# First norm and projections: modulation weights loaded by pairs of features with 1 KB rows, both token halves accumulated in six banks, values computed behind all features

## The chip, the cores and the metric

The kernel runs on one NeuronCore of a Trainium2 chip. The metric is the device time of one execution in microseconds (us). The core has five engines, each with an instruction stream of its own: TensorE (PE, matmuls, with its weight loads shown as PEld), VectorE (DVE), ScalarE (ACT), GpSimd (POOL) and SyncE (SP, which issues nearly all transfers). Tiles live in the on-chip memory with 128 partitions; matmuls write to eight banks of accumulators, each 128 partitions by 512 float32 elements.

## The reference

A trunk of two layers over 1024 tokens with 1024 channels, in float32. Each layer norms its input, modulates it, mixes tokens (layer 0: attention with a forget gate; layer 1: gated linear attention), and then runs a norm, a modulation and a gated feed-forward part. The change lies in the first norm, the first modulation and the first projections of layer 0:

```python
def rms_norm(x, g):
    y = xf * lax.rsqrt(jnp.mean(xf * xf, axis=-1, keepdims=True) + EPS)
    return (y * g).astype(x.dtype)

def modulate(h, shift, scale):
    return h * (1.0 + scale[:, None, :]) + shift[:, None, :]
...
...
def forgetting_attention(h, w_in, b_f, w_out):
    proj = h @ w_in
    q, k, v, f_logit = jnp.split(proj, [D_MODEL, 2 * D_MODEL, 3 * D_MODEL], axis=-1)
    ...
    log_f = jax.nn.log_sigmoid(f_logit.astype(jnp.float32) + b_f.astype(jnp.float32))
    cum = jnp.cumsum(log_f, axis=1).transpose(0, 2, 1)
    ...
        logits = logits + cum[:, :, qs:qe, None] - cum[:, :, None, :qe]
```

The modulation of a layer comes from `mod = c_act @ ada_w[i] + ada_b[i]`: six vectors of 1024, shift, scale and gate for the mixer and the same three for the feed-forward part. There are 16 heads of 64 channels, so a pair of heads is 128 channels.

## The kernel before, in words

**Numbers.** Every float32 matrix is held as a pair: a high part in the reduced format that TensorE takes, and a low part, the difference. A product is three matmuls, high by high, high by low and low by high (`mm3`, lines 241 to 243). A weight is loaded (`load_w`, L198), cast to its high part in two pieces on ACT (L206), and its low part is made in four pieces, three on POOL and one on DVE (L209).

**Features and tokens.** "Feature" d is a block of 128 of the 1024 channels, 0 to 7. Tokens come in two halves of 512. `xt[0]` to `xt[7]` hold x, 128 tokens each. `h` is held transposed: `hT[d]` has feature d on the partitions and tokens along the row.

**The first stage** does this:

- `load_x` fetches x, `load_ada0(d)` the first two modulation vectors' weights of feature d: two tiles, each with two transfers of 256 KB whose rows are 128 floats, 512 bytes (L288). There are 32 such transfers.
- `ss_half(hf)` norms one half of the tokens: squares with row sums on ACT (L456), the mean on DVE (L458), the power -1/2 on POOL (L459), and the scaling of each `xt` on DVE, ACT or POOL (L463, L465, L467). All four scalings of the second half are on POOL.
- `ada0_mod(d)` makes shift and scale of feature d: for features 0 to 2 half of the sum over the 1024 inputs goes on TensorE as products with `cact` (L479), the rest, and all of it for features 3 to 7, is accumulated on DVE over tiles of 256 columns (L485, L487), and its partitions are summed by a product with `ones` (L489). Then `modc` (L490) and `amul` (`make_a`, L351).
- `h_block(d, hf)` transposes x of that feature on TensorE (L496), applies scale and shift on ACT (`y_s`, L498), casts to the high part on ACT (L500), and makes the low part on DVE for even d, on POOL for odd (L501).
- `first_k(d, hf, acc)` adds feature d to three accumulators, each in a bank of its own: the forget gate `fs_b` (L508, L509), and the first query and key pair `qs_b`, `ks_b`.
- `first_v(d)` adds feature d to the values of the first token half, in two more banks, one feature behind `first_k` (`VLAG = 1`).
- `first_evac` takes the accumulators out: the gate through a sum of the gate's parts, an absolute value, an exponential and, after the second half, a logarithm, the scan over tokens (L803) and a round trip to memory from which `load_cum` (L821) brings the sums back for each head; then the query and key copies.
- `v_split` copies values out of their bank as a pair: cast on ACT (L163), difference on DVE (L164).

The first half of the tokens runs through all eight features first (the loop `for d in range(8)` with `pre(d + 1)`), with x of the second half loaded and normed at d = 4; then the second half runs through all eight. The banks of the first stage are divided by `ps_rings(5, 2, 1)`: five for accumulators (`par`), two for transposes, one for modulation products. Afterwards the banks are divided anew: two (`pj`) for projections, the others for scores, transposes and outputs of attention.

**Behind the first stage.** `run(v_half(0, 1))` computes the values of the second token half in the two `pj` banks (`vps_b`, lines 241 to 243). Then seven rounds follow: round p runs attention of head pair p (scores `s_b`, transposes, outputs `o_b`) woven with the query and key projections of pair p + 1 (`qk_b`, `qk_proj`), and in rounds 0 to 5 with half of the values of a later group. At the end of each `qk_proj` the call `ada0(3.0)` issues so much of the rest of layer 0's modulation (`ada_steps`: loads L369, accumulation on DVE in `acc_s`, L386 and L388, in steps of one unit): the other four of the six vectors, which are needed after attention.

**What sets the order.** The code is written as a sequence; a scheduler then lays the instructions out for each engine by dependences and its own estimate of when each could start, so an instruction that is written later can stand earlier on its engine. `tc.issue_after(ins)` keeps the instructions written under it behind `ins`. Rings (`Ring`, `take`) hand out slots of memory in turn: the next tile of a ring waits for the last reader of the tile that had its slot. SP issues transfers in its own order, and a transfer that waits for a slot holds up those behind it.

## Time and profile before

| | |
|---|---|
| median of 3 runs | 2428.96 us (2426.21 to 2429.33) |
| the profiled execution | 2424.66 us, of which the profile's span is 2422.8 us |
| granted TensorE clock, mean | 0.994 |
| TensorE busy | 2369.6 us (98%), 12344 matmuls |
| DVE busy | 1772.8 us (73%) |
| ACT busy | 1130.3 us (47%) |
| POOL busy | 1025.2 us (42%) |
| moved by DMA | 359.24 MB, mean 148 GB/s |

How to read the rows that follow: times are in us from the span's start. A line such as `58.93 1.33 DVE L487 ... x1` in the timeline is an instruction (or several alike, xN) with its start, its duration, engine, line of the code, operation, output tile, inputs and shape; brackets at its end give the idle time of the engine before it and what ended that wait. In rows of groups the two numbers behind the bar are the busy time in us and the mean duration of one in ns; behind the next bar stands the idle time of the engine just before them. "busy" for TensorE includes times at which it runs at a lower granted clock. The TensorE clock that is granted stands as a share of full speed.

### The profile page before, as it was taken

To read this page: it belongs to the slowest core of one execution; us is meant where nothing else is said; L and a number is where in the kernel's file an instruction comes from. 1 tells how busy PE (TensorE), PEld (TensorE's weight loads), DVE (VectorE), ACT (ScalarE), POOL (GpSimd) and SP (SyncE) were. 2 spreads that over 40 slices of the span, in tenths; PEclk is the share of its full clock that TensorE was granted. 3 is DMA by queue.
4 is the path that set the end of the run, shared out by engine and by line. 5 is a ranking of instruction groups with operands and counts; after the bars stand their busy time and mean duration, and the time that the engine had idled before them with its cause. 6 is when DMAs were issued, how large, how long until landed. Compare 5 with 4: busy or idle time off the path is not lost.

```text
span 2422.8 us, 35876 instructions
## 1 busy us (share of the span) xinstructions
PE 2369.6 (98%) x12344; PEld 2015.4 (83%) x12344; DVE 1772.8 (73%) x3044; ACT 1130.3 (47%) x2186; POOL 1025.2 (42%) x922
## 2 busy tenths in 40 slices
...
GB/s 272 80 88 107 93 115 103 91 88 105 126 96 200 169 166 174 153 181 259 228 213 176 61 126 97 114 116 168 109 92 178 157 133 154 133 169 262 226 205 148
DMA packets 348959, 359.24 MB, mean 148 GB/s; under 512 B 24221, under 2 KB 293689, under 8 KB 348777
## 3 DMA queue, kind: packets, MB, share of 16 engines
...
q14 instruction: 86, 0.70, 0.1%
...
## 4 chain that ended last, share of the span: by engine, by line
PE 81%; DVE 7%; DMA 4%; SPq 2%; ACT 2%; issue 2%; POOL 1%; DVEq 0%; POOLq 0%; ACTq 0%
PE p_b L243 16%; PE p_b L242 16%; PE p_b L241 16%; PE o_b L964 2%; PE t_b L950 2%; PE qk_b L241 2%; PE qk_b L242 2%; PE qk_b L243 2%; SPq L369 1%; DMA ad_s<-in_ada_w_dram 1%; PE s_b L919 1%; PE s_b L920 1%; PE vps_b L241 1%; PE vps_b L243 1%; PE vps_b L242 1%
## 5 line engine op out<-in xcount | busy, mean ns | idle before, releaser
L164 DVE TENSOR_TENSOR o_s<-xv_s,o_s 128x512 fp32r<-128x512 f32 (+1 forms) x376 | 321.8, 859 | 59.0 <-ACT o_s L163 58.3
L163 ACT CAST o_s<-xv_s 128x512 fp32r<-128x512 f32 (+1 forms) x376 | 217.1, 587 | 311.6 <-PE p_b L243 256.4
L242 PE MATMUL p_b<-B,o_s 128*128 128x512 f32 x608 | 236.9, 390 | 0.0
L243 PE MATMUL p_b<-B,o_s 128*128 128x512 f32 x608 | 236.5, 389 | 0.0
L241 PE MATMUL p_b<-B,o_s 128*128 128x512 f32 x608 | 235.5, 390 | 0.0
L930 POOL TENSOR_SCALAR lp_s<-lp_s,st 128x128 f32<-128x128 f32 (+7 forms) x128 | 97.5, 766 | 301.8 <-DVE st L929 260.3
L700 POOL TENSOR_TENSOR ex_s<-xv_s,xv_s 128x512 f32<-128x512 f32 (+1 forms) x64 | 86.3, 1349 | 274.8 <-DMA xv_s<-in_ffn_w_in_dram 104.0
L242 PE MATMUL p_b<-T,o_s 128*128 128x512 f32 x480 | 186.9, 389 | 0.0
L241 PE MATMUL p_b<-T,o_s 128*128 128x512 f32 x480 | 186.9, 389 | 0.0
L243 PE MATMUL p_b<-T,o_s 128*128 128x512 f32 x480 | 181.2, 390 | 0.0
L243 PEld LDWEIGHTS p_b<-B,o_s 128*128 128x128 f32 x608 | 114.1, 188 | 23.7
L242 PEld LDWEIGHTS p_b<-B,o_s 128*128 128x128 f32 x608 | 114.2, 188 | 23.6
L241 PEld LDWEIGHTS p_b<-B,o_s 128*128 128x128 f32 x608 | 114.2, 188 | 23.5
L928 ACT ACTIVATE lp_s<-lp_s,st 128x128 f32<-128x128 f32 (+7 forms) x128 | 99.3, 776 | 69.2 <-DVE st L924 66.7
L702 POOL TENSOR_TENSOR xv_s<-ex_s,xv_s 128x512 f32<-128x512 f32 (+1 forms) x64 | 84.4, 1319 | 67.2 <-DVE o_s L164 65.0
L163 ACT CAST pt_s<-t_b 128x512 fp32r<-128x512 f32 (+1 forms) x160 | 79.5, 547 | 70.4 <-PE t_b L950 69.6
L1303 DVE TENSOR_TENSOR ex_s<-ex_s,p_b 128x512 f32<-128x512 f32 x140 | 93.6, 680 | 24.2 <-PE p_b L243 24.1
L242 PEld LDWEIGHTS p_b<-T,o_s 128*128 128x128 f32 x480 | 90.1, 188 | 18.7
L241 PEld LDWEIGHTS p_b<-T,o_s 128*128 128x128 f32 x480 | 90.1, 188 | 18.7
L243 PEld LDWEIGHTS p_b<-T,o_s 128*128 128x128 f32 x480 | 90.1, 188 | 18.6
L164 DVE TENSOR_TENSOR pt_s<-t_b,pt_s 128x512 fp32r<-128x512 f32 (+1 forms) x160 | 96.3, 631 | 11.1 <-ACT pt_s L163 10.9
L924 DVE CUSTOM_DVE_ANT_0 lp_s<-s_b,cum_s 128x512 f32<-128x512 f32 (+3 forms) x128 | 72.2, 569 | 41.3 <-PE t_b L950 23.7
...
## 6 DMA issues: line engine op xcount, KB each, us to landing
...
ada_s<-in_ada_w_dram SPq DMA_DIRECT2D x128, 128.0 KB, 2.8
...
```

Of the source, the lines that this page charges most:

```text
L163: nc.scalar.copy(hi, src)
L164: nc.vector.tensor_sub(lo, src, hi.bitcast(F32))
L241: nc.tensor.matmul(ps, ah, bh, start=start, stop=False)
L242: nc.tensor.matmul(ps, ah, bl, start=False, stop=False)
L243: nc.tensor.matmul(ps, al, bh, start=False, stop=stop)
L700: nc.gpsimd.tensor_add(s1, a21, a22)
L702: nc.gpsimd.tensor_sub(a11, s1, a11)
L924: nc.vector.tensor_tensor_reduce(lp[:, k0:k1], ps, cm[:, k0:k1], 1.0, mcur, ALU.add, ALU.min, mnew)
L928: nc.scalar.activation(lp, lp, AF.Exp, bias=mcur, scale=-1.0, accum_out=st[:, qi, 2:3])
L930: nc.gpsimd.tensor_scalar(lp, lp, st[:, qi, 3:4], 1.0, op0=ALU.mult, op1=ALU.mult)
L950: nc.tensor.transpose(tp[:, i, :], lps[qi][:, psl(2 * b + jj)], ident)
L1303: nc.vector.tensor_add(d, d if src is None else dest(G, src), ps)
```

## The change

- The weights of the first modulation are loaded by pairs of features (`d2`, 0 to 3): a tile has two of the eight input blocks, and its rows are 256 floats, 1 KB. The pieces are 256 KB as before, and there are 32 as before. Their order on SP's queue changes: x of the second half comes behind pair 1, ahead of pairs 2 and 3; both value weights come behind pair 3.
- Shift and scale are made for a pair at a time. Only pair 0 has a part on TensorE (two of eight input blocks); the rest is accumulated on DVE, in tiles of 512 columns, into two `acc2` views that take one slot from the `wst` ring.
- The first accumulation of a pair is kept behind the last low part of an even feature that was written before it (`lo_ins`), the first product of pairs 1 to 3 behind the last TensorE instruction written before it, the squares of the second half behind ACT's last instruction, and the splits of the value weights behind the last instruction of each engine at that point (`split_after`).
- The banks are divided 6, 1, 1. Both token halves have their three accumulators at once, and the loop runs over pairs: pair d2 of the first half, then pair d2 - 1 of the second half. The last pair of the second half comes at the end.
- `first_v` is gone: the values of both halves are computed by `v_half(0, 0)` and `v_half(0, 1)` in the two `pj` banks, behind all features.
- The scalings of the second half are spread as those of the first: two on DVE, one on ACT, one on POOL.
- The rest of layer 0's modulation is left out of round 0 and issued at 3.5 instead of 3.0 for each call from round 1 on.

```diff
@@ -201,13 +201,21 @@
         flat = lambda t: t.rearrange("p k m -> p (k m)")
         hi, lo, rw = flat(w.hi), flat(w.lo), flat(raw)
         n = kk * m
+        def behind(e):
+            return tc.issue_after(split_after[e]) if split_after else ExitStack()
         for i in range(2):
             cs = slice(i * n // 2, (i + 1) * n // 2)
-            nc.scalar.copy(hi[:, cs], rw[:, cs])
+            with behind("A"):
+                nc.scalar.copy(hi[:, cs], rw[:, cs])
         for i in range(4):
             cs = slice(i * n // 4, (i + 1) * n // 4)
-            (nc.gpsimd if i < 3 else nc.vector).tensor_sub(lo[:, cs], rw[:, cs], hi[:, cs].bitcast(F32))
+            with behind("G" if i < 3 else "D"):
+                (nc.gpsimd if i < 3 else nc.vector).tensor_sub(lo[:, cs], rw[:, cs], hi[:, cs].bitcast(F32))
         return w
+    split_after = {}
 
     def load_w16(src, name, ws=ws):
 
@@ -270,23 +278,25 @@
     mrows = take(4)
     adr = Ring(big, adr_sl + mrows[1:] + acc_sl + s1_sl)
     mrows = Views(mrows[:1], 8, [P], "mrows").v
-    wst = Ring(big, take(6))
-    par, tp0, mp0 = ps_rings(5, 2, 1)
+    wst = Ring(big, take(5))
+    acc2 = Views(take(1), 2, [2, 256], "acc2")
+    par, tp0, mp0 = ps_rings(6, 1, 1)
 
     xt = [xr([P, D], F32, f"xt{t}") for t in range(8)]
 
     def load_x(t):
         nc.sync.dma_start(xt[t], x[0, psl(t), :])
 
-    adaw = ada_w.rearrange("l (k p) (j d m) -> l p k j d m", p=P, j=6, m=P)
+    adaw = ada_w.rearrange("l (k p) (j d m) -> l p k j d m", p=P, j=6, m=256)
     araw = {}
 
-    def load_ada0(d):
-        for kh in range(2):
-            t = adr([P, 4, 2, P], F32, f"adas{d}{kh}")
+    def load_ada0(d2):
+        for kq in range(4):
+            t = adr([P, 2, 2, 256], F32, f"adas{d2}{kq}")
             for j in range(2):
-                nc.sync.dma_start(t[:, :, j, :], adaw[0, :, 4 * kh:4 * kh + 4, j, d, :])
-            araw[(d, kh)] = t
+                nc.sync.dma_start(t[:, :, j, :], adaw[0, :, 2 * kq:2 * kq + 2, j, d2, :])
+            araw[(d2, kq)] = t
 
     load_x(0)
     rows2 = mrows[1][0:32]
@@ -312,7 +322,8 @@
     wq0 = load_w(W[:, 0:P], "wq0", wst)
     wk0 = load_w(W[:, D:D + P], "wk0", wst)
     load_ada0(1)
-    load_ada0(2)
+    for t in range(4, 8):
+        load_x(t)
 
 
     crep = [yv.v[3][0:8, psl(t)] for t in range(4)] + [mrows[4][0:16, :], mrows[5][0:16, :]]
@@ -450,45 +461,50 @@
 
     hT = new_h("h0")
 
-    def ss_half(hf):
+    def ss_half(hf, after=None):
         for t in range(4 * hf, 4 * hf + 4):
             sq = sqr([P, D], BF16, f"sq{t}")
-            nc.scalar.activation(sq, xt[t], AF.Square, accum_out=ssx[:, t:t + 1])
+            with tc.issue_after(after) if after else ExitStack():
+                nc.scalar.activation(sq, xt[t], AF.Square, accum_out=ssx[:, t:t + 1])
         cs = slice(4 * hf, 4 * hf + 4)
         nc.vector.tensor_scalar(rstd[:, cs], ssx[:, cs], 1.0 / D, EPS, op0=ALU.mult, op1=ALU.add)
         nc.gpsimd.tensor_tensor(rstd[:, cs], rstd[:, cs], mhalf[:, 0:4], op=ALU.pow)
         for t in range(4 * hf, 4 * hf + 4):
             r = rstd[:, t:t + 1]
-            if hf == 0 and t % 2 == 0:
+            if t % 2 == 0:
                 nc.vector.tensor_scalar(xt[t], xt[t], r, None, op0=ALU.mult)
-            elif hf == 0 and t == 1:
+            elif t % 4 == 1:
                 nc.scalar.activation(xt[t], xt[t], AF.Copy, scale=r)
             else:
                 nc.gpsimd.tensor_scalar(xt[t], xt[t], r, 1.0, op0=ALU.mult, op1=ALU.mult)
 
-    VLAG, XD = 1, 4
-    NPE = (4, 4, 4, 0, 0, 0, 0, 0)
-    def ada0_mod(d):
-        npe = NPE[d]
-        mp = mp0([P, 2], F32, f"mp{d}")
-        part = lambda k: araw[(d, k // 4)][:, k % 4]
-        for j in range(2):
-            for k in range(npe):
-                nc.tensor.matmul(mp[:, j:j + 1], part(k)[:, j, :], cact[:, k:k + 1], start=k == 0 and j == 0,
-                                 stop=k == 7 and j == 1)
-        if npe < 8:
-            acc = sm.tile([P, 2, P], F32, tag="t1k", name=f"acc0{d}")
+    NPE = (2, 0, 0, 0)
+    def ada0_mod(d2, after_d, after_p):
+        npe = NPE[d2]
+        mp = mp0([P, 2, 2], F32, f"mp{d2}")
+        part = lambda k: araw[(d2, k // 2)][:, k % 2]
+        acc = acc2()
         for k in range(npe, 8):
             if k == npe:
-                nc.vector.tensor_scalar(acc, part(k), cact[:, k:k + 1], None, op0=ALU.mult)
+                with ExitStack() as es:
+                    if after_d:
+                        es.enter_context(tc.issue_after(after_d))
+                    nc.vector.tensor_scalar(acc, part(k), cact[:, k:k + 1], None, op0=ALU.mult)
             else:
                 nc.vector.scalar_tensor_tensor(acc, part(k), cact[:, k:k + 1], acc, op0=ALU.mult, op1=ALU.add)
-        for j in range(2 if npe < 8 else 0):
-            nc.tensor.matmul(mp[:, j:j + 1], acc[:, j, :], ones, start=npe == 0, stop=npe == 0 or j == 1)
-        nc.vector.tensor_add(modc[:, 0, 0:2, d], mp, vec[:, d:d + 16:8])
-        make_a(0, 0, slice(d, d + 1))
+        prods = [(j, i, part(k)[:, j, psl(i)], cact[:, k:k + 1]) for j in range(2) for i in range(2) for k in range(npe)]
+        prods += [(j, i, acc[:, j, psl(i)], ones) for j in range(2) for i in range(2)]
+        for n, (j, i, w, v) in enumerate(prods):
+            with ExitStack() as es:
+                if after_p and n == 0:
+                    es.enter_context(tc.issue_after(after_p))
+                nc.tensor.matmul(mp[:, j, i:i + 1], w, v, start=n == 0, stop=n == len(prods) - 1)
+        ds_ = slice(2 * d2, 2 * d2 + 2)
+        nc.vector.tensor_add(modc[:, 0, 0:2, ds_], mp,
+                             vec[:, 0:16].rearrange("p (j d) -> p j d", j=2)[:, :, ds_])
+        make_a(0, 0, ds_)
 
     def h_block(d, hf):
         tp = tp0([P, HALF], F32, f"xp{d}{hf}")
@@ -499,6 +515,13 @@
         hi, lo = hT[d].hi[:, hsl(hf)], hT[d].lo[:, hsl(hf)]
         nc.scalar.copy(hi, y)
         (nc.gpsimd if d % 2 == 1 else nc.vector).tensor_sub(lo, y, hi.bitcast(F32))
+        if d % 2 == 0:
+            lo_ins.append(last_ins())
+    lo_ins = []
+    def last_ins():
+        return nc.cur_bb.bb.instructions[-1]
 
     def first_acc(hf):
         return [(w, par([P, HALF], F32, f"{nm}s{hf}")) for nm, w in (("f", wf), ("q", wq0), ("k", wk0))]
@@ -510,9 +533,6 @@
         for w, ps in acc[1:]:
             mm3(ps, w.hi[:, d, :], w.lo[:, d, :], hT[d].hi[:, hsl(hf)], hT[d].lo[:, hsl(hf)], d == 0, d == 7)
 
-    def last_ins():
-        return nc.cur_bb.bb.instructions[-1]
 
     sp_ins, rb_ins = [], []
     LATE1 = 7
@@ -820,55 +840,44 @@
         cums[h] = cumr([P, S], F32, f"cum{h}")
         nc.sync.dma_start(cums[h], cum_d[h].partition_broadcast(P))
 
-    vts[0] = []
     ss_half(0)
-    acc = first_acc(0)
-    vacc = [par([P, 2, 256], F32, f"vps0{tp}") for tp in range(2)]
-    def first_v(d):
-        wv = wvs[0][d // 4]
-        for tp in range(2):
-            for i in range(2):
-                ts_ = psl(2 * tp + i)
-                p_, a_ = vacc[tp][:, i, :], (hT[d].hi[:, ts_], hT[d].lo[:, ts_])
-                nc.tensor.matmul(p_, a_[0], wv.hi[:, d % 4, :], start=d == 0 and i == 0, stop=False)
-                nc.tensor.matmul(p_, a_[0], wv.lo[:, d % 4, :], start=False, stop=False)
-                nc.tensor.matmul(p_, a_[1], wv.hi[:, d % 4, :], start=False, stop=d == 7 and i == 1)
-    def pre(d):
-        ada0_mod(d)
-        if d + 3 < 8:
-            load_ada0(d + 3)
-        h_block(d, 0)
-    pre(0)
-    for d in range(8):
-        if d == 0:
-            feed.depth = 1
-            wvs[0] = [feed.next()]
-        if d == 2:
-            wvs[0].append(feed.next())
-        if d < 7:
-            pre(d + 1)
-        first_k(d, 0, acc)
-        if d >= VLAG:
-            first_v(d - VLAG)
-        if d == XD:
-            for t in range(4, 8):
-                load_x(t)
-            ss_half(1)
-    for d in range(8 - VLAG, 8):
-        first_v(d)
-    first_evac(0, acc)
-    acc = first_acc(1)
-    for tp in range(2):
-        v_split(0, tp, vacc[tp])
-    h_block(0, 1)
-    for d in range(8):
-        if d < 7:
-            h_block(d + 1, 1)
-        first_k(d, 1, acc)
-    first_evac(1, acc)
+    accs = [first_acc(hf) for hf in range(2)]
+    def last_of(e):
+        return next(i for i in reversed(nc.cur_bb.bb.instructions) if i.engine == ENG[e])
+    def blocks(d2, hf):
+        for d in (2 * d2, 2 * d2 + 1):
+            h_block(d, hf)
+    def firsts(d2, hf):
+        for d in (2 * d2, 2 * d2 + 1):
+            first_k(d, hf, accs[hf])
+    feed.depth = 1
+    for d2 in range(4):
+        ada0_mod(d2, lo_ins and lo_ins[-1], d2 and last_of("P"))
+        if d2 < 2:
+            load_ada0(d2 + 2)
+        blocks(d2, 0)
+        if d2 == 1:
+            ss_half(1, last_of("A"))
+        if d2 == 3:
+            split_after.update((e, last_of(e)) for e in "ADG")
+            wvs[0] = [feed.next(), feed.next()]
+        firsts(d2, 0)
+        if d2 == 0:
+            continue
+        if d2 == 3:
+            first_evac(0, accs[0])
+        blocks(d2 - 1, 1)
+        firsts(d2 - 1, 1)
+    blocks(3, 1)
+    firsts(3, 1)
+    split_after.update((e, last_of(e)) for e in "ADG")
+    first_evac(1, accs[1])
     def v_half(g, half):
 
         if g not in vts:
@@ -893,7 +902,8 @@
             ps = pj([P, HALF], F32, f"qk{i}{p}{hf}")
             yield from proj(ps, wt, hT, hf)
             (k_evac if i else q_evac)(ps, qkt[p], hf)
-        ada0(3.0)
+        if p > 1:
+            ada0(3.5)
 
     oTs = {}
 
@@ -1008,6 +1018,7 @@
     acc0 = acc_r([P, 2, HALF], F32, "acc0")[:, 0, 0:256]
     for j in (2, 3, 4, 5):
         ada0.q.append(ada_steps(0, j, acc0, wr, 4, 0))
+    run(v_half(0, 0))
     run(v_half(0, 1))
     for p in range(7):
         parts = [qk_proj(p + 1, 0), qk_proj(p + 1, 1)]
```

## The prediction

> **What bounds the kernel now.** I read the page first, then the busy time by stretch over the start of the kernel, then the timeline there. The page gives the profiled execution's span and shows TensorE as the chain that ends last.
>
> ```profile
> span 2422.8 us, 35876 instructions
> PE 81%; DVE 7%; DMA 4%; SPq 2%; ACT 2%; issue 2%; POOL 1%; DVEq 0%; POOLq 0%; ACTq 0%
> ```
>
> The change lies in the first norm and the projections behind it, so what matters is how much of that stage is not TensorE work. The table by stretch (busy us of PE, PEld, DVE, ACT, POOL with their counts, then granted clock, DMA share, GB/s):
>
> ```profile
> 22.00:38.00 16.00, 15.34 (x70) 13.67 (x71) 11.81 (x27) 3.83 (x6) 5.36 (x7) 0.79 1.16 299
> 38.00:56.80 18.80, 17.28 (x108) 14.73 (x107) 15.67 (x39) 10.85 (x19) 7.00 (x8) 1.00 1.12 304
> 56.80:66.90 10.10, 2.57 (x11) 1.51 (x9) 9.44 (x13) 1.78 (x4) 7.95 (x8) 0.59 0.16 40
> 66.90:78.90 12.00, 11.98 (x61) 10.65 (x61) 8.04 (x15) 7.42 (x13) 2.56 (x2) 0.78 0.56 166
> 78.90:108.20 29.30, 29.28 (x189) 26.21 (x187) 11.51 (x19) 20.37 (x35) 5.04 (x5) 1.00 0.07 19
> 108.20:110.80 2.60, 0.00 (x0) 0.00 (x0) 2.60 (x4) 1.26 (x3) 2.60 (x1) 1.00 0.01 3
> 130.00:140.00 10.00, 7.78 (x65) 7.45 (x64) 6.44 (x17) 4.72 (x12) 1.79 (x3) 1.00 0.22 68
> 165.00:465.00 300.00, 295.70 (x1966) 261.78 (x1965) 237.34 (x621) 183.52 (x404) 111.06 (x154) 1.00 0.34 104
> ```
>
> Up to 56.8 us the DMA engines are full (share 1.12 to 1.16). Then comes a hole: 2.57 us of TensorE work in 10.1. From 66.9 to 108.2 TensorE is full, and from 165 it is full again (295.7 of 300). What can be won is therefore the hole, the pause at 108.2 and the 2.2 us missing at 130 to 140. The timeline says who makes them:
>
> ```profile
> 56.25 4.99 POOL L467 TENSOR_SCALAR xt_s<-xt_s,rstd 128x1024 f32<-128x1024 f32 x4
> 58.17 0.84 DVE L386 TENSOR_SCALAR acc_s<-ada_s,c 128x256 f32<-128x256 f32 x1 [0.29 <-DMA ada_s<-in_ada_w_dram]
> 58.93 1.33 DVE L487 SCALAR_TENSOR_TENSOR acc<-adas_s,cact,acc 128x256 f32<-128x256 f32 x1
> 64.19 0.99 PE L489 MATMUL mp_b<-ones,acc 128*128 128x1 f32 x4 [4.80 <-DVE acc L487]
> 110.83 0.47 PE L241 MATMUL qk_b<-h0h,w_h_s 128*128 128x512 f32 x1 [2.65 <-DVE v_s L164]
> 132.82 0.48 DVE L388 SCALAR_TENSOR_TENSOR acc_s<-ada_s,c,acc_s 128x256 f32<-128x256 f32 x1 [3.41 <-DMA ada_s<-in_ada_w_dram]
> 134.48 0.62 PE L964 MATMUL o_b<-pt_s,v_s 128*128 128x256 f32 x3 [2.22 <-DVE pt_s L164]
> ```
>
> The modulation of feature 7 is late on DVE, because the layer's other modulation (L386, L388) has slipped between its steps and the four scalings on POOL slow DVE (1.33 us for an operation that takes 0.48 alone). At 132.8 DVE stands 3.41 us for a load of that same other modulation, and TensorE with it. The pause before 110.83 is the copying of values out of the two `pj` banks.
>
> **The change part by part.** I place the changed kernel on the same clock and ask when `qk_b` starts (110.83 now), with everything ahead of it done in both. A granted clock of 1.00 stands in the rows below unless I say otherwise.
>
> *Loads.* The queue is the same up to x3, which lands at 10.74. The 32 pieces of 256 KB stay 32 pieces, with half the rows.
>
> ```profile
> 10.74 1.06 ACT L456 ACTIVATE sq_s<-xt_s 128x1024 bf16<-128x1024 f32 x1 [0.16 <-DMA xt_s<-in_x_dram]
> 18.61 1.14 ACT L206 CAST wk0h_s<-wk_s 128x512 fp32r<-128x512 f32 x2 [0.67 <-DMA wk_s<-in_fox_w_in_dram]
> 25.92 0.35 DVE L485 TENSOR_SCALAR acc<-adas_s,cact 128x256 f32<-128x256 f32 x1 [1.71 <-DMA adas_s<-in_ada_w_dram]
> 30.95 1.14 ACT L206 CAST wv_0h_s<-wv_s 128x512 fp32r<-128x512 f32 x2 [1.44 <-DMA wv_s<-in_fox_w_in_dram]
> GB/s 0 199 198 344 180 360 361 308 244 227 281 300 291 291 290 291 291 290 293 336 300 294 294 291 300 333 297 289 292 358 405 412 378 305 291 203 181 203 149 17
> ```
>
> From wk (18.61) to the end of feature 2's weights (25.92) eight pieces with 512 B rows land: 0.91 us each. Then four more such (3.65 us) and the 512 KB of `wv`, whose rows are 1 KB, end at 30.95: 1.4 us, 0.70 us per 256 KB. The x rows (4 KB) run at about 405 GB/s, 1.3 us each (the last line, in slices of 1.5 us). So 0.75 us a piece, between 0.70 and 0.91: pair 0 is in at 16.7, the forget, query and key weights at 21, pair 1 at 27, x4 to x7 at 32, pair 2 at 38, pair 3 at 44, the value weights at 47. SP now passes x4 to x7 ahead of pairs 2 and 3, and both value loads behind everything; they were in the middle. The Trainium skill (DMA: Bandwidth & Descriptors, Specifications) gives 512 B as the least transfer for line rate, by which the wider rows bring nothing; the rows here show 0.91 against 0.70, and by its rule pair 0 would be in 1.3 us later.
>
> *DVE work for the modulation.* 8 + 44 operations on 256 columns become 4 + 26 on 512, and TensorE's products with `cact` go from 24 to 8.
>
> ```profile
> L487 DVE SCALAR_TENSOR_TENSOR acc<-adas_s,cact,acc 128x256 f32<-128x256 f32 x44 | 24.6, 569 | 0.9
> L485 DVE TENSOR_SCALAR acc<-adas_s,cact 128x256 f32<-128x256 f32 x8 | 3.5, 434 | 2.2 <-DMA adas_s<-in_ada_w_dram 2.1
> L1167 DVE SCALAR_TENSOR_TENSOR B<-ya_s,modc,B 128x512 fp32r<-128x512 f32 x16 | 11.2, 744 | 0.0
> 43.13 0.50 PE L489 MATMUL mp_b<-ones,acc 128*128 128x1 f32 x4
> L498 ACT ACTIVATE y_s<-xp_b,modc,amul 128x512 f32<-128x512 f32 x16 | 12.2, 774 | 27.8 <-DVE amul L351 24.5 <-PE xp_b L496 3.4
> L500 ACT CAST h0h<-y_s 128x512 fp32r<-128x512 f32 x16 | 9.7, 617 | 0.2
> L456 ACT ACTIVATE sq_s<-xt_s 128x1024 bf16<-128x1024 f32 x8 | 8.4, 1056 | 3.7 <-DMA xt_s<-in_x_dram 3.5
> L463 DVE TENSOR_SCALAR xt_s<-xt_s,rstd 128x1024 f32<-128x1024 f32 x2 | 2.3, 1186 | 1.1 <-POOL rstd L459 1.1
> L459 POOL TENSOR_TENSOR rstd<-rstd,mhalf 128x4 f32<-128x4 f32 x2 | 2.0, 1025 | 16.7 <-DVE rstd L458 16.7
> ```
>
> A 512-column step takes 0.75 us undisturbed, a first one I put at 0.55 (between 0.43 and 0.74). In sum 28.1 us become 26 x 0.75 + 4 x 0.55 = 21.7 us, a gain on an engine that is not the bound. What counts is where they stand. In the order of the built program pair p's sum starts only behind the low part of the last even feature, and its `ones` products stand in TensorE's queue behind the projections before it. So a pair costs in series: sum 0.55 + 7 x 0.75 = 5.8, products 0.95 (four, two of which take 0.50), `modc` and `amul` 0.35, `y` 0.78, `h` 0.62, handovers 0.3: 8.8 us from the release of the sum to the first projection.
>
> *The chain up to the last pair.* Pair 0: scaling of x ends 15.5 as now, sum of six steps and a small split 4.6, products at half clock 1.8, a weight split and the small operations 1.0: `y` at 23, low part at 24.7. Pair 1's sum 24.7 to 30.5 (its last piece landed at 27); with products and the rest `h` of feature 2 is there at 34.2, of 3 at 35.7. The squares of x4 to x7 are ordered behind that cast on ACT: 4 x 1.18 = 4.7, `rstd` 0.2, power 1.03, two scalings on DVE 2.3: x4 to x7 are ready at 44, though they landed at 32. Behind TensorE's transposes of them stands everything else, so it pauses from 38.3 to 44.1. The low part of feature 0 of the second half is done at 46.9, and only then pair 2's sum (its weights wait since 38): 52.7. `h` of 4 at 55.5; 5, then 2 of the second half, low part at 60.2. Pair 3's sum: 66.0; `h` of feature 6, and with it the last projections, at 69.
>
> *From there to `qk_b`.*
>
> ```profile
> 93.79 0.40 PE L508 MATMUL fs_b<-h0h,fw_s 128*128 128x512 f32 x1
> 95.62 0.28 PE L242 MATMUL vps_b<-wv_4l_s,h0h 128*128 128x256 f32 x1
> 101.05 0.28 PE L241 MATMUL vps_b<-wv_0h_s,h0h 128*128 128x256 f32 x1
> 107.29 0.28 PE L243 MATMUL vps_b<-wv_4h_s,h0l 128*128 128x256 f32 x1
> 31.65 2.34 POOL L209 TENSOR_TENSOR wv_0l_s<-wv_s,wv_0h_s 128x256 fp32r<-128x256 f32 x3 [2.62 <-ACT wv_0h_s L206]
> 98.19 0.58 ACT L223 COPY ze_s<-fs_b 16x512 f32<-16x512 f32 x1 [4.91 <-PE fs_b L509]
> 107.32 0.42 DVE L164 TENSOR_TENSOR v_s<-vps_b,v_s 128x256 fp32r<-128x256 f32 x1
> ```
>
> A feature's projections take 1.83 us (eight matmuls, 93.79 to 95.62), a value product 0.12 us (52 of them, 101.05 to 107.29). At 69 there remain 6 features (11.0), 5 sets of transposes (2.3), all 192 value products (23.0) and the first scores (0.65): 36.9 us. Three stalls come on top. The value weights are split behind the last casts of the first half, on ACT and then POOL (2.34 us for three quarters): 1.4 us before the cover of other products is there. The third value product needs the bank whose copying out stands on DVE behind the forget gate's chain: 98.19 to 107.74 now, 9.6 us and one more cast of 0.37, against 69 products (8.3 us) that cover it: 1.7 us. Sum: 69 + 36.9 + 3.1 = 109.0 us, 1.8 us ahead of 110.83. That last stall replaces the 2.65 us of now, since `qk_b` finds its bank free.
>
> What the sum leaves out: POOL slows DVE where both run (0.569 on average against 0.48 undisturbed for the same step above). A low part or a weight split on POOL of about 1.35 us falls on each of pairs 1 to 3; at 1.75 times the duration that is 0.6 to 1.0 us per pair, 2.2 us. And the clock: from 69.12 to 72.10 below seven matmuls take 0.43 us each instead of 0.23, after the hole.
>
> ```profile
> 69.12 0.63 PE L242 MATMUL qs_b<-h0l,wq0h_s 128*128 128x512 f32 x1
> 72.10 0.47 PE L242 MATMUL qs_b<-h0l,wq0h_s 128*128 128x512 f32 x1
> ```
>
> After the pause of 5.8 us I expect the same once, 1.7 us, of which pair 2's sum hides most (TensorE waits 2.35 us for it); I take 0.5. So `qk_b` at 111.7, 0.9 us later than now. Bounds: 0.70 and 0.68 for the DVE step and no disturbance give 107.5, everything disturbed and half clock after each pause 118.
>
> *The other modulation.* Its steps leave the first stage and the first of the seven attention rounds, and go at 3.5 instead of 3.0 a call into the other six. The 2.2 us at 134.48 vanish; what returns is a sixth more of it in rounds in which TensorE is busy 98.6% and DVE 79%: bounds 0 and 2 us, taken 0.5, nearest to the 4.3 us that all causes cost TensorE in those 300 us.
>
> *At no cost.* Six banks for `par` and one each for transposes and modulation: the transposes of the next feature wait for ACT's `y`, which the projections of the one before cover (1.83 against 0.78 + 0.62). `wst` loses a slot to `acc2`; its value halves go to slots of their own as before.
>
> Sum: +0.9 - 2.2 + 0.5 = -0.8 us. The profiled execution took 2424.66 us (2422.8 and 1.9 around it), 4.3 below the median of the runs, 2428.96. So 2423.9 in a profile like that, **2428 us** in the median: no change that can be measured (0.2%, 4.9 us, is about what a measurement of this kernel can tell).
>
> **The rivals.**
>
> *Faster, about 2421 us.* The pauses are shorter than I make them: steps undisturbed (-2.2), the clock never drops (-0.5), the value weights are split in time (-1.4), and without the other modulation the first rounds run freer than the 2.2 us (another 2 us). Sum -6.9, some 2422, or 2421 with 0.68 us a step. For it: DVE has 6.4 us less to do, the gate chain ends 5 us earlier against the scores. Against it: the pauses at pairs 1 to 3 are in the order, not in the load.
>
> *Slower, about 2435 us: the half clock.* After each pause TensorE runs about 3.6 us at half clock, 1.7 us lost. Places: from the start up to 38 (0.79 granted in 22 to 38 now, in spite of 15.34 us of work in 16), after 38.3 to 44.1, before pair 2 and before pair 3: four times 1.7, 6.8 us, of which nothing is hidden if DVE is disturbed as well. Then `qk_b` starts at 111.2 + 6.8 = 118, sum +7.2 - 2.2 + 0.5 = +5.5 to +7 us. It decides from the point where the pauses at pairs 2 and 3 (3.6 us each with the products in them) count as idle. The Trainium skill (TensorE: Matmul & The Clock Gate, Part 1: The HAM clock gate) says that an idle window of about 3.4 us brings the half clock and a busy one takes it away; the hole and the 3.6 us after it agree. By that rule the pause of 5.8 us drops the clock for certain and those of pairs 2 and 3 may.
>
> *The change does not do what it says:* the rows of 1 KB bring nothing, 0.91 us a piece. Then pair 0 is 1.3 us later, pair 1's sum only 0.5, since it waits for DVE by then: +1 us, 2429, inside the forecast.
>
> **How the numbers follow.** The forecast (with the last rival) 0.37, faster 0.33, slower 0.30. The forecast's own range is 2424 to 2433; the cases on both sides hold most of the chance, so the range reaches past both by what the six later rounds may add, a microsecond each, since another order of the start shifts what collides in them: 2421 - 6 = 2415 to 2435 + 6 = 2441.
>
> **What would show it.** TensorE idle some 6 us around 38 to 44 behind POOL or DVE `xt`, and 2 us in front of the `ones` products of pairs 2 and 3; no L388 step before 165; `qk_b` between 109 and 114; no gap of 2 us near 134. It is wrong if pair 2's sum is not behind the second half's scaling, if half-clock rows stand after 55, or if the rounds from 165 on differ by more than 2 us.

## The result

| | before | changed |
|---|---|---|
| median | 2429.47 us (2426.21 to 2430.78, 6 runs) | 2439.23 us (2435.11 to 2441.93, 6 runs) |
| profiled execution | 2424.66 us, span 2422.8 us | 2439.18 us, span 2437.2 us |
| granted clock, mean | 0.994 | 0.991 |

The ratio is 1.0039, with a 95% interval of 1.0026 to 1.0052: the change costs 9.8 us, where 2428 us and no measurable change had been forecast. The page of the changed kernel, its span and its chain of waits by engine:

```profile
span 2437.2 us, 35771 instructions
...
PE 78%; DVE 9%; DMA 5%; ACT 3%; issue 2%; SPq 2%; POOL 1%; DVEq 0%; POOLq 0%; ACTq 0%
```

TensorE still ends last, with more of the chain on DVE, ACT and DMA. The stretches that the prediction showed of before, now of the changed kernel (busy us of PE, PEld, DVE, ACT, POOL with counts, granted clock, DMA share, GB/s):

```profile
22.00:38.00 16.00, 12.06 (x47) 9.21 (x47) 9.29 (x14) 6.91 (x11) 6.41 (x8) 1.00 1.07 368
38.00:56.80 18.80, 10.53 (x42) 7.59 (x41) 10.03 (x14) 7.70 (x12) 4.50 (x4) 0.82 0.57 174
56.80:66.90 10.10, 9.81 (x43) 7.82 (x43) 4.40 (x6) 5.02 (x8) 2.69 (x2) 0.83 0.00 0
66.90:78.90 12.00, 8.35 (x32) 6.83 (x33) 5.34 (x10) 5.03 (x9) 3.08 (x5) 0.72 0.00 1
78.90:108.20 29.30, 28.48 (x205) 26.55 (x204) 13.77 (x22) 22.20 (x36) 9.03 (x11) 1.00 0.19 55
...
130.00:165.00 35.00, 34.15 (x248) 31.34 (x247) 23.48 (x66) 20.29 (x47) 15.79 (x23) 1.00 0.24 73
165.00:465.00 300.00, 293.80 (x1944) 260.52 (x1943) 241.99 (x624) 178.61 (x393) 107.51 (x148) 0.99 0.35 108
```

The hole at 57 to 67 us is filled, but 8.3 us are missing at 38 to 56.8 and 3.7 at 67 to 79, both with a clock below 1. From 130 to 165 TensorE is fuller than before (34.15 against 32.78 us), from 165 to 465 emptier (293.80 against 295.70). TensorE's timeline names the waits:

```profile
43.50 0.78 PE L512 MATMUL xp_b<-ident,xt_s 128*128 128x128 f32 x2 [3.98 <-DVE xt_s L475]
...
54.68 1.05 PE L503 MATMUL mp_b<-ones,acc_s 128*128 128x1 f32 x8 [1.60 <-DVE acc_s L496]
...
70.66 1.73 PE L503 MATMUL mp_b<-ones,acc_s 128*128 128x1 f32 x8 [2.28 <-DVE acc_s L496]
...
113.58 0.40 PE L249 MATMUL qk_b<-h0h,w_h_s 128*128 128x512 f32 x1
```

`qk_b` starts at 113.58 instead of 110.83, only 2.75 us later. So most of the 14.5 us between the two profiled executions arises behind the stage that was changed. To see where, I took the starts of the same matmuls in both traces and the median of their differences in stretches of 20 us, on the clock of the kernel before (us later than in the first profile of before; minus is earlier; the rows below the first are the experiments' profiles):

| kernel | 200 | 300 | 400 | 480 | 560 | 600 | 660 | 1000 | 1600 | 2000 | 2400 |
|---|---|---|---|---|---|---|---|---|---|---|---|
| changed | 0.4 | 1.0 | 1.2 | 5.3 | 5.7 | 10.2 | 10.2 | 11.8 | 11.9 | 15.1 | 14.4 |
| before_again | 0.1 | -0.1 | -0.1 | -0.1 | 0.2 | 0.3 | 0.3 | 2.0 | 1.9 | 4.2 | 3.8 |
| after_again | 3.2 | 3.7 | 3.8 | 7.7 | 7.7 | 11.5 | 11.5 | 13.2 | 14.2 | 15.9 | 15.3 |
| after_pace3 | 4.9 | 4.8 | 4.7 | 4.8 | 6.1 | 7.3 | 7.3 | 10.7 | 10.7 | 10.9 | 10.2 |
| before_pace35 | -4.7 | -4.2 | -3.9 | -0.2 | 0.0 | 0.2 | 0.2 | 0.2 | 1.1 | 2.7 | 2.8 |
| before_skip0 | -5.1 | -5.1 | -6.5 | -4.6 | -2.5 | -2.0 | -1.6 | 0.0 | 0.5 | 1.9 | 2.1 |
| after_pad | 2.7 | 3.2 | 3.2 | 6.9 | 6.6 | 6.8 | 6.8 | 6.8 | 5.8 | 7.3 | 7.6 |
| after_warm | 2.5 | 3.0 | 2.8 | 6.3 | 6.1 | 6.0 | 6.0 | 9.2 | 8.8 | 9.5 | 9.2 |
| after_sq | -5.6 | -5.1 | -4.7 | -0.2 | -0.2 | 4.2 | 4.2 | 5.8 | 8.6 | 6.5 | 5.3 |
| after_sq_acc | -6.2 | -5.7 | -5.3 | -1.3 | -1.5 | 2.8 | 2.8 | 4.4 | 4.9 | 4.3 | 3.4 |
| mix35 | -6.8 | -4.0 | -3.4 | -0.7 | -1.2 | -1.1 | -1.1 | -1.1 | 1.2 | 2.5 | 2.1 |
| mix_skip30 | -7.4 | -7.4 | -8.8 | -6.6 | -3.8 | -3.3 | -3.0 | -2.9 | -4.3 | -2.9 | -3.5 |
| mix30 | -7.1 | -7.3 | -7.3 | -7.4 | -7.6 | -7.6 | -7.6 | -4.3 | -4.0 | -1.0 | -1.1 |

The changed kernel's lag has three steps: 4 us between 400 and 480, 4.5 between 560 and 600, and some 4 behind 660. Each is taken up below. (A value stands for the 20 us from the time at the head of its column.)

**The step at 430.** The timeline of the changed kernel, rows of SP, DVE and TensorE:

```profile
420.56 10.61 SPq L380 DMA_DIRECT2D ada_s<-in_ada_w_dram  x12
...
426.51 3.60 DVE L399 SCALAR_TENSOR_TENSOR acc_s<-ada_s,c,acc_s 128x256 f32<-128x256 f32 x7
...
433.43 0.48 DVE L399 SCALAR_TENSOR_TENSOR acc_s<-ada_s,c,acc_s 128x256 f32<-128x256 f32 x1 [1.98 <-DMA ada_s<-in_ada_w_dram]
...
436.15 0.90 PE L960 MATMUL t_b<-ident,lp_s 128*128 128x128 f32 x3 [2.26 <-POOL lp_s L940]
```

Three loads of the other modulation, twelve pieces, stand in a row on SP; DVE works through seven steps, then stands 1.98 us for a load, the reciprocals for POOL's `lp_s` stand behind that, and TensorE waits 2.26 us. In the kernel before the same transposes follow without a wait:

```profile
431.98 0.52 PE L950 MATMUL t_b<-ident,lp_s 128*128 128x128 f32 x3
```

**The step at 586.** Attention's output of a group is written to memory (`oT_d`) and read back (`or_s`) for the output projection. The timeline (rows of SP, ACT and TensorE), and below it the DMA view of 574.4 to 581.5 us (queue; then issues with KB and us to landing), all of the changed kernel:

```profile
574.45 0.48 SPq L1001 DMA_DIRECT2D oT_d<-oT_s  x1
...
581.49 0.34 SPq L1047 DMA_DIRECT2D or_s<-oT_d  x1
...
585.06 1.04 ACT L163 CAST ohh<-or_s 128x1024 fp32r<-128x1024 f32 x1 [3.68 <-DMA or_s<-oT_d]
...
586.64 0.58 PE L974 MATMUL o_b<-pt_s,v_s 128*128 128x256 f32 x1 [2.40 <-ACT pt_s L163]
```

```profile
q1 hardware_dynamic: 672, 1.05, 43.5%
q8 instruction: 1, 0.02, 0.8%
...
oT_d<-oT_s SPq DMA_DIRECT2D x1, 512.0 KB, 7.0
```

The same view of before, from the write's issue to that of the reading back (568.71 to 573.75):

```profile
q1 hardware_dynamic: 672, 1.05, 65.9%
...
oT_d<-oT_s SPq DMA_DIRECT2D x1, 512.0 KB, 5.0
```

The write landed 7.0 us after its issue; in before it was 5.0. One packet lies in it that before does not have there: 16 KB of instructions on queue 8, from 578.39 to 579.33 us in the trace. ACT's cast of `or_s`, which has to come first, is late, `pt_s` behind it too, and TensorE waits 2.40 us.

**The steps behind 660** have no wait. These are the stretches at half clock of the changed kernel, and below them the window of 3.41 us ahead of four of them:

```profile
43.53:50.35 6.82, 5.29 (x15) 3.80 (x16) 4.47 (x6) 3.01 (x5) 1.99 (x2) 0.50 0.69 198
57.18:60.59 3.41, 3.41 (x11) 2.82 (x12) 0.69 (x1) 1.87 (x3) 0.95 (x1) 0.50 0.00 0
70.83:77.66 6.83, 5.51 (x20) 4.74 (x21) 1.01 (x3) 3.79 (x7) 1.72 (x3) 0.50 0.00 1
436.06:439.47 3.41, 3.32 (x13) 3.03 (x14) 3.27 (x9) 1.03 (x2) 0.04 (x1) 0.50 0.36 97
586.25:593.07 6.82, 5.63 (x17) 4.66 (x18) 5.29 (x11) 4.24 (x9) 2.11 (x3) 0.50 0.47 146
692.06:695.47 3.41, 3.41 (x10) 2.64 (x9) 0.00 (x0) 0.00 (x0) 0.87 (x1) 0.50 0.00 0
1344.01:1347.42 3.41, 3.41 (x18) 3.41 (x18) 0.00 (x0) 1.14 (x2) 0.38 (x1) 0.50 0.40 116
1780.91:1787.74 6.83, 6.83 (x23) 5.86 (x23) 0.16 (x1) 0.00 (x0) 1.02 (x1) 0.50 0.00 1
```

```profile
432.65:436.06 3.41, 1.25 (x10) 0.97 (x8) 2.63 (x7) 1.88 (x4) 0.91 (x1) 1.00 0.56 156
582.84:586.25 3.41, 1.40 (x12) 1.16 (x10) 0.11 (x1) 1.19 (x2) 0.00 (x0) 1.00 0.35 142
688.65:692.06 3.41, 3.41 (x30) 3.32 (x30) 0.16 (x1) 0.47 (x1) 1.13 (x2) 1.00 0.20 78
1777.50:1780.91 3.41, 3.41 (x27) 3.18 (x26) 0.19 (x1) 0.85 (x2) 2.60 (x2) 1.00 0.73 287
```

Two follow the waits just named, in whose windows TensorE was busy for 1.25 and 1.40 of 3.41 us. The others follow windows in which it was busy throughout, with matmuls of one column:

```profile
688.23 3.40 PE L547 MATMUL sp_b<-ones,ss_s 128*128 128x1 f32 x30
```

Every stretch at half clock is 3.41 us long or a whole multiple of it. Half of such a stretch is lost where TensorE is the bound, 1.7 or 3.4 us. (The stretch at the very end of the run, where TensorE has run out of work, is left out here and below.) Before has the same thirty matmuls at 678.03 us, and no half clock there.

### The profile page after: what moved, and what is told of

Same layout as the page of the kernel before. It is cut to its first block, busy times and chain, and to the rows that moved or that the text cites. A ratio compares the mean times of both kernels' runs of the same rounds, so it can differ in the third digit from the quotient of the medians.

```text
span 2437.2 us, 35771 instructions
## 1 busy us (share of the span) xinstructions
PE 2374.2 (97%) x12312; PEld 2016.6 (83%) x12312; DVE 1767.6 (73%) x3016; ACT 1132.9 (46%) x2187; POOL 1023.1 (42%) x919
## 4 chain that ended last, share of the span: by engine, by line
PE 78%; DVE 9%; DMA 5%; ACT 3%; issue 2%; SPq 2%; POOL 1%; DVEq 0%; POOLq 0%; ACTq 0%
PE p_b L249 16%; PE p_b L251 15%; PE p_b L250 15%; PE o_b L974 2%; PE t_b L960 2%; SPq L380 1%; PE qk_b L249 1%; PE qk_b L250 1%; PE qk_b L251 1%; DMA ad_s<-in_ada_w_dram 1%; PE vps_b L249 1%; PE vps_b L250 1%; PE vps_b L251 1%; PE s_b L929 1%; PE s_b L930 1%
## 5 line engine op out<-in xcount | busy, mean ns | idle before, releaser
L164 DVE TENSOR_TENSOR pt_s<-t_b,pt_s 128x512 fp32r<-128x512 f32 (+1 forms) x160 | 96.1, 631 | 12.2 <-ACT pt_s L163 11.8
L214 POOL TENSOR_TENSOR w_l_s<-w__s,w_h_s 128x256 fp32r<-128x256 f32 x90 | 70.6, 812 | 76.4 <-ACT w_h_s L210 61.7
```

The costliest lines, as they stand in the source:

```text
L164: nc.vector.tensor_sub(lo, src, hi.bitcast(F32))
L214: (nc.gpsimd if i < 3 else nc.vector).tensor_sub(lo[:, cs], rw[:, cs], hi[:, cs].bitcast(F32))
```

## The experiments

Ratios are to the kernel before on the same chip, with 95% intervals. All profiles of the table above come from these runs.

**Both kernels again.** No edit.

> The changed kernel unaltered, for a second profile. In the first one the lag behind the kernel before is 2.75 us at the start of qk_b, about 0.4 us at 200 us, 5.7 at 550, 10.2 at 600 and 14.4 at the end; most of the later steps are stretches at half clock (436 to 439, 586 to 593, 692 to 695, 1344 to 1347, 1781 to 1788 us). Theory 'grid': the clock is decided in windows of 3.41 us that run freely against the kernel, so the repeat has the same waits but half-clock stretches in other places; its time is 2435 to 2442, and stretches after 200 us sum to anything from 3.4 to 27 us. Theory 'order': the new order of the start brings these stretches at fixed places; then the repeat shows the same five within a microsecond.

> The kernel before unaltered, for a second profile. Theory 'grid': its profile showed only one half-clock stretch after 80 us (3.4 us at 1332) and was 4.8 us below the median, so a repeat shows two or more, and 2426 to 2431 us; qk_b starts within 1 us of 110.8. Theory 'order': again one alone, at 1332, and 2424 to 2426 in the profile.

Measured: after_again 2438.20 us, 1.0038 (1.0024 to 1.0052); before_again 2428.37 us, 0.9997 (0.9988 to 1.0007). Half clock in after_again behind 200 us stands at 591, 694, 1342 to 1349, 1410 and 1782 to 1789 us, no longer at 436. In before_again it came where the first profile had none:

```profile
681.55:684.96 3.41, 3.41 (x10) 2.73 (x10) 0.16 (x1) 0.00 (x0) 1.02 (x1) 0.50 0.02 5
...
1770.40:1777.23 6.83, 6.83 (x22) 5.67 (x22) 0.16 (x1) 0.00 (x0) 1.02 (x1) 0.50 0.00 0
```

The same code, with the same thirty matmuls at 678.32 us, and the clock halves. In both profiles of before the boundaries of the stretches are whole multiples of 3.413 us apart, but they lie 1.7 us apart between the profiles, counted from each span's start. So the windows run freely against the kernel, and "grid" holds for what lies behind 660. The Trainium skill (TensorE: Matmul & The Clock Gate, Part 1: The HAM clock gate) says that the window is 3413 ns and free-running; the lengths and the two profiles agree. "Order" is not empty either: four of the five places came back in after_again within 5 us, and all fourteen profiles have half clock between 1320 and 1350 us. The places belong to the code, mostly to its one-column matmuls; whether the clock falls there, and for how long, changes. The lag that a profile gains behind 660 goes from -0.5 us (mix_skip30) to +6.5 (mix30), before_again gains 3.5. That is luck of one execution: 4.2 us of the changed kernel's 14.4 are such, and before's first profile happened to have one stretch alone. I take it to be in the medians of both kernels alike, which is argued and not shown; at 660 us the lags of the changed kernel's two profiles, 10.2 and 11.5, are near the 9.8 between the medians.

after_again shows two more things. The step at 430 is there again (3.8 to 7.7) without half clock, so the wait makes it and not the clock:

```profile
438.94 0.55 PE L960 MATMUL t_b<-ident,lp_s 128*128 128x128 f32 x3 [2.48 <-POOL lp_s L940]
```

And the start differs between the two profiles of the changed kernel: `qk_b` at 113.58 and 115.68, the lag at 200 us 0.4 and 3.2. The key weight landed later; ACT's cast of it, first and second profile:

```profile
20.85 1.14 ACT L210 CAST wk0h_s<-wk_s 128x512 fp32r<-128x512 f32 x2 [0.62 <-DMA wk_s<-in_fox_w_in_dram]
```

```profile
23.34 1.14 ACT L210 CAST wk0h_s<-wk_s 128x512 fp32r<-128x512 f32 x2 [2.35 <-DMA wk_s<-in_fox_w_in_dram]
```

DVE's `amul` stands behind this weight's low part, so the first `y` came 2.6 us later. A lag at the start is therefore known to some 3 us only, and the first profile is on the low side.

**The other modulation's pace alone, in both kernels.**

```diff
 # after_pace3 (in the changed kernel)
-        if p > 1:
-            ada0(3.5)
+        ada0(3.0)
 # before_pace35 (in the kernel before)
-        ada0(3.0)
+        if p > 1:
+            ada0(3.5)
 # before_skip0 (in the kernel before)
-        ada0(3.0)
+        if p > 1:
+            ada0(3.0)
```

> The changed kernel with the other modulation paced as before (3.0 a call, from round 0). Theory 'pacing' (3.5 in rounds 1 to 6 makes new waits for TensorE there, at 436 and 586): ratio to before falls from 1.004 to 1.000 to 1.002, and round 0 has a wait of 2 us more. Theory 'start' (the stage itself is what costs): ratio stays at 1.003 to 1.005. My forecast's own sum says +2 us against the changed kernel, 1.0047.

> The kernel before with the other modulation left out of the first stage and round 0 and paced 3.5 from round 1 on. Theory 'pacing': slower than before by 3 to 7 us, ratio 1.001 to 1.003. Theory 'start': the hole at 57 to 66 us shrinks (its steps stood between those of feature 7) and the 2.2 us at 134 vanish: 2 to 5 us faster, ratio 0.998 to 0.999.

> The kernel before with the other modulation left out of the first stage and round 0, and at 3.0 a call afterwards. At 3.5 it was 4.7 us ahead at 200 us and had lost all of it by 440, mostly at 430, where a call issues four steps in a row, their loads are late and TensorE waits 1.7 us and then has half clock. Theory 'lump': at 3.0 no call issues more than three steps, the 4.7 us stay, ratio 0.998 to 0.9985. Rival 'amount': the same sum of steps in fewer rounds costs the same, ratio 0.9995 to 1.000.

Measured: after_pace3 2434.71 us, 1.0029 (1.0017 to 1.0041); before_pace35 2428.35 us, 0.9995 (0.9985 to 1.0005); before_skip0 2427.36 us, 1.0002 (0.9990 to 1.0014). The first two lie between what "pacing" and "start" had, the third is nearest to "amount". The medians tell little apart; the table tells more. In before_pace35 the deferral gains 4.7 us by 200, as "start" had it, and 3.7 of them are lost between 400 and 480, at the wait at 430 that "pacing" named; after 560 nothing is left. after_pace3 has no step at 430. In before_skip0, at 3.0 a call, TensorE has no wait for a load at 430; the step there is smaller (2 us, with 1.22 us of wait for DVE's `QB`), but new waits at 486 to 491 us, with 6.8 us of half clock behind them, take most of the rest. "Lump" falls: at 3.0 four loads stand in a row (394 to 410 us), no fewer than the three at 430, and TensorE does not stand for them. That it depends on where the loads meet DVE's other work is what remains, and no run isolates it. So leaving the modulation out of round 0 only moves its cost. With the same pace in both, the changed stage itself costs 5.2 us (1.0 less -4.2, at 300), 7.9 by after_again (3.7), and 4.8 by after_pace3 against before.

**The order at the start.**

```diff
 # after_sq
-            ss_half(1, last_of("A"))
+            ss_half(1)
 # after_sq_acc: that, and
-    ada0_mod(d2, lo_ins and lo_ins[-1], d2 and last_of("P"))
+    ada0_mod(d2, None, d2 and last_of("P"))
```

> The changed kernel with the squares of x4 to x7 no longer kept behind ACT's casts; they then stand ahead of the h of features 2 and 3. Theory 'order at the start': x4 to x7 are scaled at 36 to 38 us instead of 44.9, TensorE's pause of 4.0 and the two of 0.7 and 0.9 behind it go, pair 2's sum ends at 48 to 50 instead of 54.6, qk_b starts at 107.5 to 110 instead of 113.6, ratio 1.001 to 1.003. Rival 'clock': the pauses only move and the half-clock stretches stay, qk_b at 112 to 114.

> The same, and the sums of pairs 1 to 3 no longer kept behind the last low part of an even feature. Theory 'order at the start': pair 2's sum ends soon after its weights (38 to 42 us), pair 3's by 50, the waits in front of the products of pairs 2 and 3 (1.6 and 2.3 us, with 1.3 each for modc, amul and y) go with their half clock, qk_b at 102 to 106, ratio 0.998 to 1.001. Rival: DVE's longer queue ahead of the scalings makes x4 to x7 as late as before (44), and nothing is gained, qk_b at 112 to 114.

Measured: after_sq 2433.76 us, 1.0023 (1.0012 to 1.0033), `qk_b` at 107.3; after_sq_acc 2430.35 us, 1.0020 (1.0010 to 1.0029), `qk_b` at 106.5. The squares alone take 6.1 us off the lag at 300 (8.8 against after_again), more than the whole cost of the stage: the pause before the transposes of x4 to x7 was its cause, and "clock" falls. The time falls as expected, by 0.0016, but the intervals of the changed kernel and of after_sq overlap, so the trace carries this and not the median. The sums' order brings 0.6 us more instead of the 4 or more expected, and the ratio missed its 0.998 to 1.001; the waits in front of the products went, but TensorE then waits 2.55 us for the `y` of pair 3 at 53.74. Both still lose 4.3 to 4.4 us at 580.

**The load of instructions.**

```diff
 # after_pad, behind firsts(1, 0)
+            pad = mp0([P, 16], F32, "pad")
+            for i in range(16):
+                with tc.issue_after(last_of("P")):
+                    nc.tensor.matmul(pad[:, i:i + 1], ident, ones, start=i == 0, stop=i == 15)
 # after_warm, at the same place
+            pad = mp0([P, HALF], F32, "pad")
+            for i in range(16):
+                with tc.issue_after(last_of("P")):
+                    nc.tensor.matmul(pad, wq0.hi[:, 0, :], hT[0].hi[:, 0:HALF], start=i == 0, stop=i == 15)
```

> The changed kernel with 16 matmuls of one column added in TensorE's pause before the transposes of x4 to x7 (39 to 43.5 us), which write a bank that nobody reads. Float32 matmuls count double in the trace, so these are the 32 matmuls by which the change has fewer. In the changed kernel a 16 KB load of instructions (578.4 to 579.3 us) falls between the writing of attention's output to memory and its reading back, which is issued 7.0 us after the write instead of 5.0, TensorE then waits 2.4 us and the clock halves for 3.4 to 6.8 us. Theory 'code load': that load follows TensorE's instruction count, so with the 32 restored it stands some 7 us earlier or later, the read is issued 5.0 us after the write, the wait is about 1 us, and the lag behind the kernel before grows by under 1 us at 580 instead of 4; the total falls by 2 to 4.5 us, ratio 1.001 to 1.003. Rival 'other traffic': the read back stays at 7.0 us and the ratio at 1.004. The start of qk_b stays at 113 to 116.

> The changed kernel with 16 matmuls of 512 columns added in the pause before the transposes of x4 to x7, into a bank that nobody reads. With 16 matmuls of one column there (after_pad) TensorE was as busy in the records, and the clock still halved from 45.2 to 52.0 us. Theory 'wide work keeps the clock': no half-clock stretch between 40 and 55 us, h of the second half's feature 0 to the low part as before, and pair 2's sum, the next thing on the path, starts at 47 to 48 us as in the changed kernel, so qk_b gains 0 to 1 us (113 to 114). Rival 'busy by the records is enough or does not matter': half clock again at 43 to 51. The load of instructions moves by half as much as in after_pad, to some 575 us, ahead of the read back: the wait at 586 is between 1 and 2.4 us.

The DMA view of after_pad from the issue of the write (575.3) to that of the reading back (580.4), then TensorE's timeline there:

```profile
q1 hardware_dynamic: 672, 1.05, 64.7%
...
oT_d<-oT_s SPq DMA_DIRECT2D x1, 512.0 KB, 5.0
```

```profile
586.88 0.75 PE L979 MATMUL o_b<-pt_s,v_s 128*128 128x256 f32 x4 [0.99 <-DVE pt_s L164]
```

No instruction packet is in it (it now comes at 572.85), the write takes 5.0 us again, the wait is 0.99, and there is no half clock at 586: the lag stays at 6.6 to 6.8 from 560 to 600. In the trace "code load" holds. after_warm, with half as many added instructions, has the packet at 574.06, a microsecond ahead of the write, and no step at 580 either. Over all profiles the step of 3.7 to 4.5 us is there in the four in which the packet falls 2.9 to 3.9 us behind the issue of the write (changed, after_again, after_sq, after_sq_acc: 6.3 to 7.0 us to landing), a smaller one (1.2 us) in after_pace3, where it falls 1.8 us behind it, and at most 0.5 us in the others. In the time it shows less well: after_pad 2434.64 us, 1.0038 (1.0023 to 1.0053, four runs), where 1.001 to 1.003 had been expected and the rival had 1.004, so its time cannot tell; and after_warm 2434.40 us, 1.0024 (1.0016 to 1.0033). The Trainium skill (Runtime: NRT & Kernel Launch, Instruction fetch mechanics) says that an engine's sequencer fetches its instructions itself over a DMA queue in blocks of 16 KiB and that the cost is mostly hidden; the 16 KB packets agree, and here one was not hidden.

The two kernels also measure what keeps the clock. After_pad, then after_warm, by stretch:

```profile
40.50:44.00 3.50, 3.50 (x33) 3.42 (x31) 0.43 (x2) 2.12 (x5) 1.24 (x2) 1.00 1.10 349
41.74:45.15 3.41, 3.22 (x27) 2.90 (x26) 1.58 (x3) 1.80 (x3) 2.38 (x2) 1.00 1.09 347
45.15:51.98 6.83, 5.15 (x16) 3.75 (x16) 4.48 (x6) 2.80 (x4) 2.00 (x2) 0.50 0.44 122
```

```profile
41.50:55.10 13.60, 10.62 (x49) 7.70 (x48) 8.87 (x11) 5.26 (x9) 4.17 (x3) 1.00 0.52 155
```

With matmuls of one column TensorE is busy 3.50 of 3.50 us, and 3.22 of 3.41 in the window ahead of the half clock, and the clock halves all the same; with 512 columns it stays. All fourteen profiles say the same. From 120 us on I counted, for each window of 3.41 us at full clock, how long TensorE was busy with matmuls of more than one column. Half clock followed all 43 windows with 1.44 us or less, 29 of which were filled to the end with one-column matmuls; it followed 9 of the 22 windows with 1.50 to 1.86 us, and none with more. That also explains the thirty matmuls at 678 us: in before a window's boundary cuts through them, which leaves 1.78 and 1.94 us of other work on its two sides, and in before_again one window has nearly all of them and 0.34 us of other work.

Keeping the clock brought no time in after_warm: pair 2's sum on DVE comes next. `qk_b` came at 115.5 instead of the 113 to 114 expected; at 60 us after_warm is 1.9 us behind the changed kernel's first profile, of which 1.1 stand since the first `y`; it has half clock from 34.7 to 41.5 where the latter has none, and it stays 2 behind up to 280.

**Together.** after_sq_acc with more of pairs 0 and 1 on TensorE, at three paces:

```diff
-    NPE = (2, 0, 0, 0)
+    NPE = (4, 2, 0, 0)
 # mix35: no more; mix_skip30: ada0(3.0) under "if p > 1"; mix30: ada0(3.0) in every round
```

> after_sq_acc with four and two of eight input blocks of pairs 0 and 1 on TensorE (8 + 8 more matmuls by the code, 32 in the trace's count), pace 3.5 from round 1 as in the changed kernel. Theory 'code load': the load of instructions moves away from the writing of attention's output, the 4.3 us that after_sq_acc loses at 580 go, and the lag at 600 us is that at 560: -1.5 to -3 us against the kernel before; ratio 0.999 to 1.000. Rival: the collision returns with another transfer, ratio 1.002 as in after_sq_acc.

> mix35 with 3.0 a call from round 1 on. From before_skip0: the lead of the start (6 us at 200) holds to 420 and is lost only by half in the last rounds. Theory: lead 3 to 5 us at 660, ratio 0.998 to 0.999. Rival 'amount': the lead is gone by 600, ratio 1.000.

> mix35 with 3.0 a call from round 0 on, as in the kernel before. Theory 'amount' (the steps of the other modulation cost some 4.7 us wherever they stand in attention): the same time as mix35 within 2 us, with the wait in round 0 or 1 instead of that at 430. Rival 'place': 3 to 5 us slower than mix_skip30.

Measured: mix35 2426.82 us, 0.9994 (0.9984 to 1.0005); mix_skip30 2421.16 us, 0.9977 (0.9968 to 0.9985); mix30 2423.50 us, 0.9980 (0.9971 to 0.9988). mix35 has no step at 580, and against after_sq_acc the ratio falls by 0.0026, some 6 us; the lag at 560 is the same within 0.3. mix_skip30 and mix30 cannot be told apart and beat both kernels, before by 5 to 6 us: at 660 mix30 has the whole lead of its start (7.6 us), mix_skip30 3.0, behind new waits at 485 to 490 and half clock. So "place" falls, which had mix30 3 to 5 us behind mix_skip30 (2.3 by the medians, 0.0003 or 0.7 us by the ratios). "Amount" does not hold either, which had it within 2 us of mix35; it is 3.3 us faster. Skipping round 0 is worth nothing that can be measured, and a pace of 3.5 costs 3 to 4 us, by ratios whose intervals just overlap.

## Why the prediction was wrong

*The loads: right.* A piece with 1 KB rows was put at 0.75 us. The stretch of the changed kernel that holds only such rows:

```profile
38.00:43.50 5.50, 1.44 (x7) 0.89 (x6) 1.07 (x3) 4.09 (x7) 1.91 (x3) 1.00 1.10 349
```

256 KB (262,144 bytes) at 349 GB/s are 0.75 us, against 291 GB/s in before's quiet slices with 512 B. The rival by which the wider rows bring nothing falls. The rule quoted from the Trainium skill (DMA: Bandwidth & Descriptors, Specifications) that 512 B are enough for line rate does not fit these two rates. The gain buys nothing: pair 2's weights are in long before DVE takes them (at 47.7 us).

*The steps on DVE: right.* The line's view of the changed kernel (count, shortest, median and longest in ns, first and last start):

```profile
L496 DVE SCALAR_TENSOR_TENSOR acc_s<-adas_s,cact,acc_s x26: 745/752/1659, 15.8 to 69.9; 128x512 f32<-128x512 f32 x26
```

0.75 us were taken. One step in each of pairs 1 to 3 takes 1.65 us while POOL makes a low part, 0.9 us a pair, in the 0.6 to 1.0 that was added for it. The factor of 1.75 behind that sum has no row in the prediction; the measured one is 2.2 (1659 against 752 ns).

*The pause: right in place and size.* It was forecast from 38.3 to 44.1 behind the squares of x4 to x7, and stands from 39.5 to 43.5 with 0.67 and 0.87 us more behind it. But I let it count as part of a stage that gained elsewhere; after_sq shows that it was the whole loss of the stage.

*The clock: mis-sized.* "I take 0.5" after one pause; the clock fell after three, at 43.5, 57.2 and 70.8. Pair 3's products took 1.73 us instead of 1.05 (pair 2's), and the eight matmuls behind them 3.4 us (74.48 to 77.88) instead of 1.83. `qk_b` came at 113.58 instead of 111.7 (115.68 in after_again), inside the bounds given (107.5 to 118).

*The stalls behind the last pair: they did not come.* The sum named three and priced two, 1.4 us for the splits of the value weights and 1.7 for copying out. From 74.48 us, where feature 6's projections start instead of at 69, to `qk_b` TensorE's timeline has no wait; its 39.1 us are the 36.9 that were added up, the half clock (1.6) and small gaps. So `qk_b` was only 1.9 us late because these 3.1 us made up for part of what the clock and the waits had cost, and that was luck.

*The first round: right.* The 2.2 us at 134 are gone: the lag falls from 2.75 at `qk_b` to 0.4 at 200.

*The other modulation: this step failed.* "... what returns is a sixth more of it ...: bounds 0 and 2 us, taken 0.5". By before_pace35 what returns is 4.7 us, all that was gained, and 3.7 of it at 430; the rounds of the changed kernel lose 5.3 us from 200 to 560. All eight profiles at 3.5 from round 1 on have the step between 400 and 480 (2.7 to 4.5 us), and the three further ones at 3.0 in every round (before_again, after_pace3, mix30) have none. I costed an amount (a sixth more work on an engine that is 79% busy) where the cost is a queue: several loads issued at once, DVE standing for one of them, and TensorE's transposes behind DVE. The row of 132.82 in the prediction, where DVE stands 3.41 us for such a load, showed the mechanism; I took its removal as a gain and did not ask where it would stand next. Two of the prediction's own signs of being wrong came true: rounds from 165 on that differ by more than 2 us, and half clock after 55.

*Not foreseen: the load of instructions.* 4.5 us, some 1.4 of it the longer wait (2.40 against 0.99) and the rest half clock, far from the edit. The prediction's allowance of a microsecond for each later round says that collisions may shift, but no term of the sum has one.

*The rival "half clock"* had the price of one stretch right (1.7 us) and its place wrong: it put all the loss ahead of `qk_b`, where `qk_b` came 1.9 us later than I took in all; the 5 us at 436 and 586 followed waits in attention.

In sum, in the first profile, in us: start and first round +0.4 (forecast -1.3), rounds behind it +5.3 (forecast +0.5), the write at 574 +4.5 (forecast none), half clock by luck behind 600 +4.2 (taken to be in the medians of both kernels). The first three are 10.2 at 660 (11.5 in after_again), against 9.8 between the medians.
